# Score blocks of a head set further apart, priority for their maxima and exponentials, and one load for four output weight tiles

## The chip, the cores and the metric

The kernel runs on one core of a Trainium2 chip. The metric is device time in microseconds for one launch. The kernel before was timed three times: 1888.44, 1889.13 and 1891.86 us, median 1889.13. One further execution was profiled: 1886.52 us, of which the profile's span covers 1884.7 us.

## The reference, cut to what matters

A two-layer backbone processes 512 latent tokens and 128 context tokens with the same weights. Layer 0 is a state-space mixer and a gated convolutional feed-forward; layer 1 is differential attention and a second feed-forward. The change concerns the attention of layer 1 and its output projection:

```python
qp, kp, vp = diff_qkv(hp, att_qkv_w[slot])                 # 128 context tokens, 8 heads, 2 maps of 64
qs, ks_, vs = diff_qkv(hs, att_qkv_w[slot])                # 512 latent tokens
qs = rope_2d(qs, tabs); ks_ = rope_2d(ks_, tabs)
k_all = jnp.concatenate([cache_k[:, slot], ks_], axis=1)   # 640 keys
...
s = jnp.einsum('bqhcd,bkhcd->bhcqk', qi, k, preferred_element_type=F32) * DA_SCALE   # per block of 128 queries
p = jax.nn.softmax(s, axis=-1)
w = p[:, :, 0] - lam * p[:, :, 1]
return jnp.einsum('bhqk,bkhd->bqhd', w.astype(v.dtype), v)
...
o = (_rms(o) * subln_g.astype(F32) * (1.0 - lam_init)).astype(o.dtype)
return o.reshape(b, l, D_MODEL) @ out_w
```

Everything is float32 and has to keep nearly that precision: each large product is made of three matmuls, high part by high part, high by low, low by high.

## The kernel before, in words

**Tiles.** Activations lie with features on the 128 partitions and the 640 tokens (512 latent, then 128 context) along the row; 1024 features are 8 feature tiles. A dense output tile (`dense`, L153) takes 48 matmuls: for each of 8 feature tiles three products (`wh` by `h` high, `wh` by `h` low, `wl` by `h` high), each in two pieces of 256 and 384 columns. After each feature tile `hook` (L76) advances the clock of ticks by one and lets the pending side tasks (Python generators) emit their next piece. A generator says with `yield n` how many ticks it wants to wait. So the text of the program is: dense tiles of the weights in one fixed sequence, and between their feature tiles whatever side task is due. A scheduler then orders each engine's instructions from that text: it keeps dependencies and prefers what came earlier in the text, or what stands under a priority block, among what it takes to be ready. Each engine then runs its list strictly from front to back.

**Weights.** `prefetch` (L119) loads weight units of up to 1024 columns into four buffers; `cast` (L127) makes the high part `whi` on ACT and the low part `wlo` on DVE, one unit ahead of its use, in three rotating buffers. `whi` of a unit can only be written when the unit three earlier has been read for the last time.

**One head.** For head `hd` the dense sequence has the tiles q, k and v (`attention`, L1160). The three tiles of head 0 are computed together beforehand (`start_tiles`, tile name `st`). ACT copies each out of PSUM (`att_evac` L1025, `att_v` L993), DVE rotates q and k (`att_rope`). `att_head` (L1060) then computes the context scores (tile `sp`, 128x128 for two maps) and four score blocks of 128 queries by 640 keys for two maps (tile `sl`, 12 matmuls). For each map DVE takes the row maximum (`sm`, L1070), ACT the exponential (tile `e`), and `combine` joins both maps into weights `w`. `att_tail` (L1114) transposes the weights (`wpt`, `wt`), splits them into `wTh` on ACT and `wTl` on DVE, multiplies with the values (`ov`, `op`), squares the result (`osq`) and takes the sum of squares (`ms`).

**PSUM.** Six of eight banks form three slots of two banks (`psd`, L66). The dense tile in progress holds one. A score block takes the other two, one for each map, and gives each back when its exponential has read it. So a dense tile that begins while a block is held starts only when the first exponential is done, and a block starts only when both slots are free. `hold` (L1018) also makes the first matmuls of a block wait for the exponentials and copies noted in `self.held`.

**Spacing.** The ticks between blocks stand in `att_head`: after `combine` of the context scores 5 (L1092; 3 in the last head), then after each block 2, and between blocks 1, 3 and 1 (L1111), so that blocks start 3, 5 and 3 ticks apart. `attention` drains the task of the previous head after the k tile (L1170): what is left of it is emitted there without further dense tiles between.

**After the heads.** `project_out` makes the first 768 input features of the first five output tiles (weights of 768 columns), and `project_last` (L289) the rest of these five (256 columns each, one load and one cast for each tile) and the last three full tiles. `attention` passes `range(6, 8)` as `ks` there. The second feed-forward follows with `start_tiles`.

Of the kernel before, what the change touches and what calls it, by code (L numbers as in the profile page):

```python
# [18 lines left out]
P = 128  # L19
D = 1024  # L20
# [25 lines left out]
class Step:  # L46
# [72 lines left out]
    def prefetch(self, upto):  # L119
        while len(self.wraw) <= min(upto, len(self.units) - 1):  # L120
            u = len(self.wraw)
            ap, n = self.units[u]
            r = self.pw.tile([P, 1024], F32, tag="raw", name=f"raw{u}", bufs=RAW)
            self.nc.sync.dma_start(r[:, :n], ap)
            self.wraw[u] = r
# [163 lines left out]
    def project_last(self, h, ks, g, nextnorm, ks_last=None, parts="AB"):  # L289


        self.norm_begin()
        for i in range(KT - 3):
            ps = self.dense_ps("po")
            self.dense(ps, self.nextw(), ks, h)
            for hf in "AB":
                self.gate_add(i, ps, g, hf)
                self.norm_sq(i, hf)
        ks = ks_last or ks
        if self.modtask:  # L300
# [671 lines left out]
    def att_consts(self, pool):  # L972
# [4 lines left out]
        lv = t([P, 256], "lv")  # L977
        nc.sync.dma_start(lv, a["lam"])
        ls = t([P, 2], "ls")
        lj = t([P, 64], "lj")  # L980
# [6 lines left out]
        nc.vector.tensor_scalar(self.nlam, self.nlam, -LAM_INIT, None, ALU.add)  # L987
        self.sg = t([P, 2], "sg")
        nc.sync.dma_start(self.sg[:, 1:], a["subg"])
        nc.vector.tensor_scalar(self.sg[:, 1:], self.sg[:, 1:], 1.0 - LAM_INIT, None, ALU.mult)  # L990
        nc.vector.tensor_scalar(self.sg[:, :1], self.sg[:, 1:], 3.0 / 8, None, ALU.mult)

    def att_v(self, ps, hd, vs, pool):  # L993

        nc = self.nc
        x = self.slot("f", f"v{hd}", bufs=NF)
        self.held["evac"] = self.act(x, ps[:, PO:PO + T], AF.Copy)
        hi = pool.tile([P, NCH, P], F32R, tag="vh", name=f"vh{hd}", bufs=2)
# [26 lines left out]
    def att_evac(self, ps, hd, name, pool):  # L1025

        x = self.slot("f", f"{name}{hd}", bufs=NF)[:, :TS]
        p = pool.tile([P, TP], F32, tag=f"{name}p", name=f"{name}p{hd}", bufs=2)
        self.act(x, ps[:, PO:PO + TS], AF.Copy)
        self.held["evac"] = self.act(p, ps[:, PO + TS:PO + T], AF.Copy, scale=DA_SCALE if name == "q" else 1.0)  # L1030
        return x, p
# [28 lines left out]
    def att_head(self, hd, qp, kp, qs, k, vs, o, pool):  # L1060
# [7 lines left out]
        def softmax(s, n, m, st):  # L1068
            e = self.slot("f", f"e{m}", bufs=NF)
            nc.vector.tensor_reduce(st[:, m:m + 1], s, AX.X, ALU.max, negate=True)  # L1070
            self.held["exp"] = self.act(e[:, :n], s, AF.Exp, bias=st[:, m:m + 1], accum_out=st[:, 2 + m:3 + m])
            return e
# [18 lines left out]
        combine(w, TP, *em, st)  # L1091
        yield 3 if last else 5  # L1092
        ws = []
        for b in range(4):
# [15 lines left out]
            if b < 3:  # L1110
                yield ((1, 1, 1) if last else (1, 3, 1) if hd else (1, 3, 3))[b]  # L1111
        self.tails[hd] = self.add(self.att_tail(hd, w, ws, vs, o, pool), 1 if last else 2)

    def att_tail(self, hd, w, ws, vs, os_, pool):  # L1114
# [11 lines left out]

        def av(kc, hi, lo):
            self.mm(py, vh[:, kc, :], hi, kc == 0, False)
            self.mm(py, vh[:, kc, :], lo, False, False)
# [3 lines left out]
        for kc in range(NCH):  # L1133
# [5 lines left out]
            self.act(hi, pm, AF.Copy)  # L1139
            self.tt(lo, pm, hi.bitcast(F32), ALU.subtract)  # L1140
            if prev:
                av(kc - 1, *prev)
            prev = hi, lo
            yield 1 if hd == 7 else 2
# [57 lines left out]
    def weight_units(self):  # L1202
# [29 lines left out]
    def run(self):  # L1232
# [27 lines left out]
        with tc.tile_pool(name="att", bufs=1) as pool:  # L1260
            self.att_consts(pool)
            self.attention(hs[2], norm(1, 1, hs[3]), pool)
# [105 lines left out]
```

## Time and profile before

| what | us |
|---|---|
| median of three runs | 1889.13 |
| profiled execution | 1886.52 |
| span of its profile | 1884.7 |
| PE busy / PEld (weight loads) busy | 1839.6 / 1744.8 |
| DVE busy / ACT busy | 1369.5 / 955.1 |
| attention, from the first q tile of head 1 to the end of `po` | 1050.65 to 1399.02 |

PE is the TensorE's stream of matmuls, PEld its weight loads, DVE the VectorE, ACT the ScalarE, SPq the queue from which loads are issued. Times within the span are microseconds from its start. In a timeline row the columns are start, duration, engine, source line, operation, out and in by tile name, shape and count; the bracket at the end is idle time of that engine before the row and what ended it. In a list of waits a row gives the waiting group, the group waited for, total us, how often, and the longest. In a table by stretches of time the columns are: the stretch, its length, busy time and instruction count of PE, PEld, DVE, ACT and POOL, the granted TensorE clock (1.00 is full), the share of the DMA engines and GB/s. Matmul rows are pipelined and overlap, so the time of a group is read from its start to the next group's start.

### The profile page before, as it was taken

To read this page: it belongs to the slowest core of one execution; us is meant where nothing else is said; L and a number is where in the kernel's file an instruction comes from. 1 tells how busy PE (TensorE), PEld (TensorE's weight loads), DVE (VectorE), ACT (ScalarE), POOL (GpSimd) and SP (SyncE) were. 2 spreads that over 40 slices of the span, in tenths; PEclk is the share of its full clock that TensorE was granted. 3 is DMA by queue.
4 is the path that set the end of the run, shared out by engine and by line. 5 is a ranking of instruction groups with operands and counts; after the bars stand their busy time and mean duration, and the time that the engine had idled before them with its cause. 6 is when DMAs were issued, how large, how long until landed. Compare 5 with 4: busy or idle time off the path is not lost.

```text
span 1884.7 us, 32852 instructions
## 1 busy us (share of the span) xinstructions
PE 1839.6 (98%) x13322; PEld 1744.8 (93%) x13322; DVE 1369.5 (73%) x2640; ACT 955.1 (51%) x1748; POOL 0.2 (0%) x4
## 2 busy tenths in 40 slices
PE   7999999999999999999999899999999999999997
PEld 5889999999899999999999888888899999999996
DVE  6699999999669999973556877778686543553554
ACT  3489697877336431441443555566456432441441
POOL 0000000000000000000000000000000000000000
PEclk9999999999999999999999899999999999999998
DMA  9836253436524557532222211111132222222211
GB/s 347 271 104 166 80 150 101 147 120 211 187 70 156 181 188 226 176 92 83 71 72 82 64 46 58 58 57 32 33 124 79 79 78 70 73 72 80 73 40 56
DMA packets 79727, 209.74 MB, mean 111 GB/s; under 512 B 9324, under 2 KB 16088, under 8 KB 79448
## 3 DMA queue, kind: packets, MB, share of 16 engines
q1 hardware_dynamic: 79000, 207.13, 34.6%
q8 instruction: 104, 1.70, 0.4%
q10 hardware_dynamic: 576, 0.52, 0.1%
q14 instruction: 47, 0.39, 0.1%
HBM read 201.66 MB, written 5.96 MB: 110 GB/s over the span
## 4 chain that ended last, share of the span: by engine, by line
PE 90%; DVE 5%; ACT 3%; DMA 2%; issue 1%; SPq 0%; DVEq 0%; ACTq 0%
PE up L104 31%; PE po L104 25%; PE z L104 6%; PE x L104 5%; PE st L104 5%; PE yp L104 3%; PE v L104 3%; PE q L104 3%; PE bc L104 3%; PE ov L104 1%; ACT e L95 1%; PE modrow L104 1%; PE in L104 1%; PE sl L104 1%; DVE sm L1070 1%; PE wt L1136 1%
## 5 line engine op out<-in xcount | busy, mean ns | idle before, releaser
L95 ACT ACTIVATE whi<-raw 128x1024 fp32r<-128x1024 f32 (+4 forms) x230 | 234.8, 1022 | 382.6 <-PE po L104 240.4
L101 DVE TENSOR_TENSOR wlo<-raw,whi 128x1024 fp32r<-128x1024 f32 (+3 forms) x229 | 269.5, 1177 | 169.6 <-ACT whi L95 164.7
L98 DVE SCALAR_TENSOR_TENSOR xr<-po,mod,xr 128x256 f32<-128x256 f32 (+2 forms) x231 | 88.8, 433 | 158.6 <-PE po L104 158.5
L104 PE MATMUL po<-mh,whi 128*128 128x256 f32 (+1 forms) x704 | 167.7, 310 | 0.0
L104 PE MATMUL po<-ml,whi 128*128 128x256 f32 (+1 forms) x704 | 167.4, 310 | 0.0
L104 PE MATMUL po<-mh,wlo 128*128 128x256 f32 (+1 forms) x704 | 167.2, 309 | 0.0
L104 PE MATMUL up<-h01h,wlo 128*128 128x256 f32 (+1 forms) x656 | 149.4, 309 | 0.0
L104 PE MATMUL up<-h11h,wlo 128*128 128x256 f32 (+1 forms) x656 | 149.4, 309 | 0.0
L104 PE MATMUL up<-h11h,whi 128*128 128x256 f32 (+1 forms) x656 | 149.4, 308 | 0.0
L104 PE MATMUL up<-h11l,whi 128*128 128x256 f32 (+1 forms) x656 | 149.3, 308 | 0.0
L104 PE MATMUL up<-h01h,whi 128*128 128x256 f32 (+1 forms) x656 | 149.3, 308 | 0.0
L104 PE MATMUL up<-h01l,whi 128*128 128x256 f32 (+1 forms) x656 | 149.3, 308 | 0.0
L104 PEld LDWEIGHTS po<-mh,whi 128*128 128x128 f32 x704 | 128.5, 188 | 0.6 <-ACT mh L95 0.4
L104 PEld LDWEIGHTS po<-mh,wlo 128*128 128x128 f32 x704 | 128.7, 188 | 0.0
L104 PEld LDWEIGHTS po<-ml,whi 128*128 128x128 f32 x704 | 128.5, 188 | 0.0
L104 PEld LDWEIGHTS up<-h11h,whi 128*128 128x128 f32 x656 | 119.3, 188 | 0.0
L104 PEld LDWEIGHTS up<-h01h,whi 128*128 128x128 f32 x656 | 119.3, 188 | 0.0
L104 PEld LDWEIGHTS up<-h01h,wlo 128*128 128x128 f32 x656 | 119.3, 188 | 0.0
L104 PEld LDWEIGHTS up<-h11l,whi 128*128 128x128 f32 x656 | 119.3, 188 | 0.0
L104 PEld LDWEIGHTS up<-h11h,wlo 128*128 128x128 f32 x656 | 119.3, 188 | 0.0
L104 PEld LDWEIGHTS up<-h01l,whi 128*128 128x128 f32 x656 | 119.2, 188 | 0.0
L98 DVE SCALAR_TENSOR_TENSOR ca<-uraw,fcw,ca 128x511 f32<-128x511 f32 (+1 forms) x176 | 85.2, 545 | 11.7 <-ACT ca L95 11.7
(497 smaller groups left out, 4327.7 us busy)
## 6 DMA issues: line engine op xcount, KB each, us to landing
raw<-in_w_up SPq DMA_DIRECT2D x88, 512.0 KB, 3.5
mw<-in_modT SPq DMA_DIRECT2D x48, 512.0 KB, 3.5
raw<-in_w_in SPq DMA_DIRECT2D x40, 512.0 KB, 5.0
rb<-rowd SPq DMA_DIRECT2D x40, 512.0 KB, 5.3
raw<-in_w_dn SPq DMA_DIRECT2D x32, 448.0 KB, 3.4
raw<-in_w_qkv SPq DMA_DIRECT2D x24, 512.0 KB, 3.6
mr<-in_mod SPq DMA_DIRECT2D x44, 256.0 KB, 5.9
mp<-in_modp SPq DMA_DIRECT2D x32, 256.0 KB, 5.4
```

The source lines that it names most:

```text
L95: return self.nc.scalar.activation(out, in_, func, **k)
L98: return self.nc.vector.scalar_tensor_tensor(out, in0, s, in1, op0, op1)
L101: return self.nc.vector.tensor_tensor(out, a, b, op)
L104: return self.nc.tensor.matmul(out, lhsT, rhs, start=start, stop=stop)
L1070: nc.vector.tensor_reduce(st[:, m:m + 1], s, AX.X, ALU.max, negate=True)
L1136: nc.tensor.transpose(pm[:, b * P:(b + 1) * P], ws[b][:, kc * P:(kc + 1) * P], self.ident)
```

## The change

Nothing of the arithmetic changes; instructions are moved.

- The ticks between blocks become 4, 4, 4 with the 2 after each block (six feature tiles apart) for heads 1 to 5; 3, 2, 2 for head 0, 2, 2, 2 for head 6, 1, 1, 1 for head 7. Head 0 waits 3 ticks in place of 5 after its context scores. The tail of heads 0 to 6 starts 4 ticks after the last block in place of 2.
- The task of the previous head is drained after the v tile, no longer after the k tile.
- Maximum and exponential of a block, and the copies of q, k, v out of PSUM, stand under `tc.high_priority()`.
- In the tail the first matmul of each product with the values also waits for `wTl`.
- The second part of the output weights comes in units of four tiles by 256 columns: two units (1024 and 256 columns) in place of five. All later units get numbers smaller by three.
- The attention's small constants are loaded before `start_tiles`, and the arithmetic on them is emitted after it.

```diff
@@ prefetch
-            self.nc.sync.dma_start(r[:, :n], ap)
+            dst = r[:, :n]
+            self.nc.sync.dma_start(dst.rearrange("p (i c) -> p i c", i=ap.shape[1]) if len(ap.shape) == 3 else dst, ap)
@@ project_last
-            self.dense(ps, self.nextw(), ks, h)
+            n = len(ks) * P
+            j = i % (1024 // n) if ks_last else 0
+            if j == 0:
+                w = self.nextw()
+            self.dense(ps, [t[:, j * n:(j + 1) * n] for t in w], ks, h)
@@ att_v
-        self.held["evac"] = self.act(x, ps[:, PO:PO + T], AF.Copy)
+        with self.tc.high_priority():
+            self.held["evac"] = self.act(x, ps[:, PO:PO + T], AF.Copy)
...
@@ att_head, softmax
-            nc.vector.tensor_reduce(st[:, m:m + 1], s, AX.X, ALU.max, negate=True)
-            self.held["exp"] = self.act(e[:, :n], s, AF.Exp, bias=st[:, m:m + 1], accum_out=st[:, 2 + m:3 + m])
+            with self.tc.high_priority():
+                nc.vector.tensor_reduce(st[:, m:m + 1], s, AX.X, ALU.max, negate=True)
+                self.held["exp"] = self.act(e[:, :n], s, AF.Exp, bias=st[:, m:m + 1], accum_out=st[:, 2 + m:3 + m])
@@ att_head
-        yield 3 if last else 5
+        yield 3 if last else 5 if hd else 3
...
-                yield ((1, 1, 1) if last else (1, 3, 1) if hd else (1, 3, 3))[b]
-        self.tails[hd] = self.add(self.att_tail(hd, w, ws, vs, o, pool), 1 if last else 2)
+                yield {0: (3, 2, 2), 6: (2, 2, 2), 7: (1, 1, 1)}.get(hd, (4, 4, 4))[b]
+        self.tails[hd] = self.add(self.att_tail(hd, w, ws, vs, o, pool), 1 if last else 4)
@@ att_tail
-        def av(kc, hi, lo):
-            self.mm(py, vh[:, kc, :], hi, kc == 0, False)
+        def av(kc, hi, lo, gate):
+            self.hold(self.mm(py, vh[:, kc, :], hi, kc == 0, False), [gate])
...
@@ attention
+        consts = self.att_consts(pool)
+        next(consts)
         o, tk, self.tails, self.held = [], [], {}, {}
         self.start_tiles(h)
+        next(consts, None)
...
-            if hd:
-                self.drain(tk[hd - 1])
             q = self.att_q(q, hd, pool)
...
             self.add(self.att_v(self.next_tile(h, "v"), hd, vs, pool), 1)
+            if hd:
+                self.drain(tk[hd - 1])
@@ weight_units
-        u += [(a["w_ao"][i, :, c:], D - c) for i in range(KT - 3)]
+        per = 1024 // (D - c)
+        u += [(a["w_ao"][i:j, :, c:].rearrange("i p c -> p i c"), (j - i) * (D - c))
+              for i in range(0, KT - 3, per) for j in (min(i + per, KT - 3),)]
```

The first place where instructions move is the PE's list around the last blocks of head 0, in the k and v tiles of head 1. Before, three of the four blocks stand close together at the end of the k tile; the names are those of the text above (`w` are the weights of a block, `kh`, `kl`, `qh`, `ql` the split keys and queries):

```order
L1119 MATMUL wpt<-cst,wp 128x128
L1136 MATMUL wt<-cst,w_11827 128x128
L104 MATMUL sl<-kh_11673,qh_11662 128x320 x4
L104 MATMUL sl<-kl_11674,qh_11662 128x320 x4
L104 MATMUL sl<-kh_11673,ql_11663 128x320 x4
L1136 MATMUL wt<-cst,w_11871 128x128
L104 MATMUL sl<-kh_11673,qh_11662 128x320 x4
L104 MATMUL sl<-kl_11674,qh_11662 128x320 x4
L104 MATMUL sl<-kh_11673,ql_11663 128x320 x4
L104 MATMUL v<-h10h_11216,whi_11772 128x256
L104 MATMUL v<-h10h_11216,whi_11772 128x384
```

Now the fourth block of head 0 stands alone at the very end of the v tile, right ahead of the q tile of head 2:

```order
L104 MATMUL v<-h10h_11230,wlo_11773 128x256
L104 MATMUL v<-h10h_11230,wlo_11773 128x384
L104 MATMUL sl<-kh_11673,qh_11662 128x320 x4
L104 MATMUL sl<-kl_11674,qh_11662 128x320 x4
L104 MATMUL sl<-kh_11673,ql_11663 128x320 x4
L104 MATMUL q<-h10h_11216,whi_11905 128x256
L104 MATMUL q<-h10h_11216,whi_11905 128x384
```

The blocks of head 0 have moved apart: behind the first stand 25 matmuls of the k tile, behind the second 12 of k and 16 of v, behind the third 32 of v.

The second place is the PE's list where the k tile of a head in the middle ends and its v tile begins. Before, the block there is the fourth of the previous head:

```order
L104 MATMUL sl<-kh_12801,qh_12790 128x320 x4
L104 MATMUL sl<-kl_12802,qh_12790 128x320 x4
L104 MATMUL sl<-kh_12801,ql_12791 128x320 x4
L104 MATMUL k<-h10h_11230,wlo_12919 128x256
L104 MATMUL k<-h10h_11230,wlo_12919 128x384
L1119 MATMUL wpt<-cst,wp 128x128
L1136 MATMUL wt<-cst,w_13018 128x128
L1136 MATMUL wt<-cst,w_13089 128x128
L1136 MATMUL wt<-cst,w_13156 128x128
L104 MATMUL v<-h10h_11216,whi_13101 128x256
```

Now it is the third:

```order
L104 MATMUL sl<-kh_12749,qh_12738 128x320 x4
L104 MATMUL sl<-kl_12750,qh_12738 128x320 x4
L104 MATMUL sl<-kh_12749,ql_12739 128x320 x4
L104 MATMUL k<-h10h_11230,whi_12878 128x256
L104 MATMUL k<-h10h_11230,whi_12878 128x384
L104 MATMUL k<-h10l_11231,whi_12878 128x256
L104 MATMUL k<-h10l_11231,whi_12878 128x384
L104 MATMUL k<-h10h_11230,wlo_12879 128x256
L104 MATMUL k<-h10h_11230,wlo_12879 128x384
L104 MATMUL ms<-osq,cst 32x160 x4
L1128 MATMUL wpt<-cst,wp 128x128
L104 MATMUL v<-h10h_11216,whi_13021 128x256
```

Between the block and the v tile now stand six matmuls of the k tile and the sums of squares, where two and the transposes stood. The fourth block has gone to the v tile, with nine matmuls of v behind it ahead of the next q tile.

The third place is ACT's list at the same spot. Before:

```order
L95 ACTIVATE whi_13344<-raw_13099 128x1024
L95 ACTIVATE wpT<-wpt 128x128
L95 ACTIVATE e_13182,sm<-sl,sm 128x640
L95 ACTIVATE e_13185,sm<-sl,sm 128x640
L95 ACTIVATE k_13205<-k 128x512
L95 ACTIVATE kp_13206<-k 128x128
```

Now:

```order
L95 ACTIVATE osq<-o_12947 128x640
L95 ACTIVATE whi_13304<-raw_13019 128x1024
L95 ACTIVATE e_13139,sm<-sl,sm 128x640
L95 ACTIVATE e_13142,sm<-sl,sm 128x640
L95 ACTIVATE k_13153<-k 128x512
L95 ACTIVATE kp_13154<-k 128x128
L95 ACTIVATE wpT<-wpt 128x128
```

In both lists the two exponentials stand behind a cast of weights; only the copy `wpT` has moved behind them. In the v tile, where the fourth block now is, its first exponential stands ahead of the cast.

More of the change, by code (lines that the diff above doesn't have):

```diff
@@ L978, in att_consts @@
         nc.sync.dma_start(lv, a["lam"])
+        self.sg = t([P, 2], "sg")
+        nc.sync.dma_start(self.sg[:, 1:], a["subg"])
+        yield
         ls = t([P, 2], "ls")
@@ L987, in att_consts @@
         nc.vector.tensor_scalar(self.nlam, self.nlam, -LAM_INIT, None, ALU.add)
-        self.sg = t([P, 2], "sg")
-        nc.sync.dma_start(self.sg[:, 1:], a["subg"])
         nc.vector.tensor_scalar(self.sg[:, 1:], self.sg[:, 1:], 1.0 - LAM_INIT, None, ALU.mult)
@@ L1028, in att_evac @@
         p = pool.tile([P, TP], F32, tag=f"{name}p", name=f"{name}p{hd}", bufs=2)
-        self.act(x, ps[:, PO:PO + TS], AF.Copy)
-        self.held["evac"] = self.act(p, ps[:, PO + TS:PO + T], AF.Copy, scale=DA_SCALE if name == "q" else 1.0)
+        with self.tc.high_priority():
+            self.act(x, ps[:, PO:PO + TS], AF.Copy)
+            self.held["evac"] = self.act(p, ps[:, PO + TS:PO + T], AF.Copy, scale=DA_SCALE if name == "q" else 1.0)
         return x, p
@@ L1069, in softmax @@
             e = self.slot("f", f"e{m}", bufs=NF)
-            nc.vector.tensor_reduce(st[:, m:m + 1], s, AX.X, ALU.max, negate=True)
-            self.held["exp"] = self.act(e[:, :n], s, AF.Exp, bias=st[:, m:m + 1], accum_out=st[:, 2 + m:3 + m])
+            with self.tc.high_priority():
+                nc.vector.tensor_reduce(st[:, m:m + 1], s, AX.X, ALU.max, negate=True)
+                self.held["exp"] = self.act(e[:, :n], s, AF.Exp, bias=st[:, m:m + 1], accum_out=st[:, 2 + m:3 + m])
             return e
@@ L1139, in att_tail @@
             self.act(hi, pm, AF.Copy)
-            self.tt(lo, pm, hi.bitcast(F32), ALU.subtract)
+            gate = self.tt(lo, pm, hi.bitcast(F32), ALU.subtract)
             if prev:
                 av(kc - 1, *prev)
-            prev = hi, lo
+            prev = hi, lo, gate
             yield 1 if hd == 7 else 2
@@ L1260, in run @@
         with tc.tile_pool(name="att", bufs=1) as pool:
-            self.att_consts(pool)
             self.attention(hs[2], norm(1, 1, hs[3]), pool)
```

## Prediction

> **What bounds the kernel now.** The page comes first: who is busy, and on which engine the chain that ended last runs.
>
> ```profile
> span 1884.7 us, 32852 instructions
> PE 1839.6 (98%) x13322; PEld 1744.8 (93%) x13322; DVE 1369.5 (73%) x2640; ACT 955.1 (51%) x1748; POOL 0.2 (0%) x4
> PE 90%; DVE 5%; ACT 3%; DMA 2%; issue 1%; SPq 0%; DVEq 0%; ACTq 0%
> ```
>
> PE sets the time nearly everywhere. The change leaves its matmuls as they are, so it can only win time in which PE waits, or runs at a reduced clock. The second view is the table by stretches, cut at the starts of q tiles: first the stretch in which head 0's blocks run (q, k, v of head 1), then three of the five heads that follow, each from its q tile to the next, then windows of 4 us at the dips of the clock.
>
> ```profile
> 1050.65:1091.62 40.97, 34.27 (x226) 30.93 (x226) 30.46 (x59) 22.50 (x49) 0.00 (x0) 0.88 0.22 71
> 1128.36:1165.08 36.72, 34.94 (x248) 30.79 (x248) 28.36 (x58) 22.44 (x48) 0.00 (x0) 1.00 0.19 59
> 1165.08:1203.36 38.28, 36.51 (x249) 32.33 (x249) 28.46 (x58) 22.43 (x48) 0.00 (x0) 0.96 0.18 55
> 1240.08:1278.34 38.26, 36.48 (x249) 32.31 (x248) 28.44 (x58) 22.42 (x48) 0.00 (x0) 0.96 0.15 46
> 1072.00:1076.00 4.00, 2.37 (x13) 1.75 (x13) 4.00 (x6) 1.79 (x3) 0.00 (x0) 0.57 0.06 16
> 1076.00:1080.00 4.00, 1.79 (x12) 1.57 (x12) 3.30 (x7) 3.01 (x6) 0.00 (x0) 0.50 0.42 131
> 1080.00:1084.00 4.00, 4.00 (x20) 3.90 (x19) 2.22 (x5) 2.31 (x5) 0.00 (x0) 0.65 0.00 0
> 1188.00:1192.00 4.00, 2.40 (x20) 1.68 (x17) 3.88 (x5) 3.42 (x8) 0.00 (x0) 1.00 0.32 82
> 1192.00:1196.00 4.00, 4.00 (x19) 4.00 (x18) 3.84 (x9) 1.61 (x5) 0.00 (x0) 0.57 0.46 147
> 1332.00:1336.00 4.00, 4.00 (x27) 2.81 (x24) 2.44 (x3) 2.53 (x6) 0.00 (x0) 0.58 0.16 49
> ```
>
> Two equal heads differ by 38.28 - 36.72 = 1.56 us and by the clock alone (0.96 against 1.00). The third view is PE's list of waits for the same three parts: head 0's stretch (three rows), the five heads to 1278.34 (three rows), the rest up to 1400.
>
> ```profile
> PE sl L104 <- ACT e L95: 3.3, 2, 2.9
> PE sl L104 <- ACT kp L95: 1.9, 1, 1.9
> PE wt L1136 <- ACT wpT L95: 1.4, 1, 1.4
> ...
> PE v L104 <- ACT e L95: 4.6, 5, 0.9
> PE wt L1136 <- ACT wpT L95: 3.4, 5, 0.7
> PE sl L104 <- ACT e L95: 0.9, 5, 0.2
> ...
> PE po L104 <- ACT e L95: 1.2, 1, 1.2
> PE v L104 <- ACT e L95: 0.9, 1, 0.9
> PE op L104 <- DVE vl L101: 0.7, 1, 0.7
> PE po L104 <- ACT whi L95: 0.6, 1, 0.6
> PE po L104 <- DVE wlo L101: 0.6, 1, 0.6
> ```
>
> Nearly all of it is PE behind an exponential (`e`). The last view is the timeline of PE, ACT and DVE at one such place, the end of a k tile.
>
> ```profile
> 1148.09 0.46 PE L104 MATMUL k<-h10h,whi 128*128 128x256 f32 x2
> ...
> 1148.97 0.46 PE L104 MATMUL k<-h10h,whi 128*128 128x256 f32 x2
> ...
> 1150.79 0.57 PE L104 MATMUL sl<-kh,qh 64*128 64x320 f32 x4 [0.19 <-ACT e L95]
> ...
> 1151.87 0.56 PE L104 MATMUL k<-h10h,wlo 128*128 128x256 f32 x2
> 1152.27 0.27 PE L1119 MATMUL wpt<-cst,wp 128*128 128x128 f32 x1
> 1153.22 0.55 PE L1136 MATMUL wt<-cst,w 128*128 128x128 f32 x3 [0.68 <-ACT wpT L95]
> 1154.68 0.39 PE L104 MATMUL v<-h10h,whi 128*128 128x256 f32 x1 [0.91 <-ACT e L95]
> ...
> 1151.96 1.04 ACT L95 ACTIVATE whi<-raw 128x1024 fp32r<-128x1024 f32 x1
> 1152.90 0.26 ACT L95 ACTIVATE wpT<-wpt 128x128 f32<-128x128 f32 x1
> 1153.74 0.79 ACT L95 ACTIVATE e<-sl,sm 128x640 f32<-128x640 f32 x1 [0.57 <-DVE sm L1070]
> ...
> 1152.09 0.88 DVE L98 SCALAR_TENSOR_TENSOR w<-e,sm,e 128x640 f32<-128x640 f32 x1
> 1152.89 1.55 DVE L1070 TENSOR_REDUCE sm<-sl 128x1 f32<-128x640 f32 x2
> 1154.35 1.22 DVE L101 TENSOR_TENSOR wlo<-raw,whi 128x1024 fp32r<-128x1024 f32 x1
> ```
>
> Read from it: one feature tile (six matmuls) takes 1148.97 - 1148.09 = 0.88 us; a block holds PE 1151.87 - 1150.79 = 1.08. From the block's end to the v tile pass 2.81 us. Two k matmuls (0.40) and three transposes (about 0.3) fill 0.7, so 2.1 are lost, and 0.19 ahead of the block: 2.3 per head. The chain that ends the wait: DVE is busy with `w` until 1152.89, maximum, exponential 0.85 us later, its 0.79, and 0.15 to the matmul. If DVE and ACT are free at the block's end, the same chain takes about 0.1 + 0.85 + 0.79 + 0.15 = 1.9 us. That is the cover which any dense tile needs that starts behind a block.
>
> **The change, part by part.**
>
> *Head 0's blocks.* They now stand 25, 28 and 32 dense matmuls apart, 3.7 us or more at 0.88 per six; each needs 1.9 us and one more exponential before the next. The listed waits (3.3 + 1.9 + 1.4 = 6.6) go, and so does the reduced clock: 2.37 x 0.43 + 1.79 x 0.50 + 4.00 x 0.35 = 3.3 us. What is late next is the fourth block, at the very end of the v tile. It waits for the exponential of head 1's context scores; on ACT that one stands behind a cast whose buffer comes free two matmuls before the tile's end. The cast takes about 0.95 (next row on ACT), the short exponential about 0.4, the ways there and back 0.35, less the last 0.3 of the tile: 1.4. Then the q tile follows at once and lacks all of the 1.9. So 9.9 go and 3.3 come: **-6.6**. Ends: -9.9 if nothing new waits; -4.0 if the two new waits cost another 1 and a dip of 1.56.
>
> *The third block, at the end of the k tile, heads 2 to 6.* The cast still stands ahead of the exponential, and its buffer is free only when four of the six k matmuls behind the block are through: 0.2 to get going + 0.59, 0.19 to ACT (about 1.0 after the block), 0.95 for the cast, 0.79 and 0.15: the v tile starts 2.85 after the block. Six matmuls (1.1 with the 0.2), sums of squares and a transpose (about 0.45) fill 1.5. Left: 1.35, where 2.3 were. If the exponential came through first, it would be 1.9 - 1.5 = 0.4.
>
> *The fourth block, nine matmuls ahead of the q tile.* Its cover is 0.2 + 9 x 0.147 = 1.5 against 1.9, a new wait of 0.4. DVE may come late by a subtraction of 1.22 (the `wlo` row): up to 1.6.
>
> *The matmul held for `wTl`.* Behind it on PE stands the dense tile, so any wait there is PE's. The subtraction must now be done too, but 12 dense matmuls (1.76) have passed since its transposes. I take 0.25 per head, between 0 and 0.7.
>
> So a head in the middle loses 1.35 + 0.4 + 0.25 = 2.0, where it lost 2.3: -0.3 each, **-1.5** for five. Ends: 0.4 + 0.4 + 0.25, -1.25 each, -6.3; on the other side 1.35 + 1.6 + 0.7 = 3.65, +1.35 each, +6.8.
>
> *The dips.* Two of five heads ran at 0.96, 1.56 us each, right after a loss of 2.1 (busy 2.40 of 4.00, then clock 0.57). The largest single gap is now 1.35: **-3.1**; between -3.1 and 0.
> The Trainium skill, "TensorE: Matmul & The Clock Gate", Part 1 (the HAM clock gate), says that the clock halves after an idle window of about 3.4 us and asks for no PE gap over about 3 us. By it no dip would stem from these gaps, this term would be 0 and the sum 3.1 smaller; the rows at 1188 and 1192 show a dip after less idling than that, and the measurement decides.
>
> *The end of the attention.* The third block of head 7 was followed by `op` and a new `po` tile, waits 0.7 + 1.2, then a dip (0.58 in 4 us, 1.7). Now two `ov`, six dense matmuls and four transposes follow it, about 1.8 against 1.9. Up to 0.5 of wait stays; and one k tile end as above, -0.3. Together 3.6 - 0.5 + 0.3: **-3.4**, between -3.9 and 0.
>
> *The weights.* Five casts of 256 columns become one of 1024 and one of 256; that is work on ACT and DVE, off PE's path. The waits of `po` for `whi` and `wlo` (0.6 + 0.6) go, since the first full tile's cast now needs only the buffer of the last 768-column unit, free five output tiles earlier. But all later units move up by three: the second and third tile of the feed-forward fall into the buffers of the last two output tiles, which are free only at the end of the projection. Two subtractions of 1.22 then stand behind that end, where the first tile's 24 matmuls (2.9) cover: I take 1.0, between 0 and 2.5. Net **-0.2**, between -1.2 and +1.3.
>
> *Constants and queues.* The loads are issued in the same place, and no PE wait in the three lists is for a load; the tails' small transfers move with their tails, with a whole tile of slack: 0.
>
> Sum: 6.6 + 1.5 + 3.1 + 3.4 + 0.2 = 14.8. The profiled execution took 1886.52 (span 1884.7 and 1.8 around it), so 1871.7 for a run like it. It lay 2.6 under the median of the three runs, 1889.13; against that median the forecast is **1874.3**.
>
> **The rivals.** A change within 0.2%, 3.8 us, cannot be told from none by a measurement of this kernel.
>
> *A, slower.* ACT and DVE run their lists from front to back; priority changes places in the list, not what is ready. For it: in the row at 1152.90 `wpT` had waited behind the cast of 1.04, and PE for `wpT`. If the exponentials at all tile ends stand behind casts and the maxima behind subtractions of 1.22, a head loses 2.5 at the k end, 2.5 at the v end, 1.4 at the gate of the fourth block and 0.25: 6.65 instead of 2.3, +4.35 for five heads = +21.8, and the three heads without a dip get one (+4.7). With head 0's -6.6 that is +19.9: 1909. Against it: ACT's list has the fourth block's first exponential ahead of the cast. It decides from (6.6 + 3.4)/5 = 2.0 more per head than now, 4.3 in all.
> The Trainium skill says on the same page (Part 1, engine queue depths) that ACT and DVE are strict FIFO and only PE reorders, weight loads alone; the row at 1152.90 agrees.
>
> *B, only head 0 gains.* Priority is void at the k ends, the dips stay, the end of the attention trades its waits for others: -6.6, 1882.5. For it: the list on ACT still has the cast first. Against it: one long loss becomes three short ones.
>
> *C, no change.* The heads lose 1.3 more each (late DVE, as in the upper end), which eats head 0's gain: 1889. DVE is busy 28.4 of 36.7 us per head, so a shorter head leaves it less room.
>
> **How the numbers follow.** Forecast (1865 to 1880) 0.58, B 0.22, C 0.09, A 0.07, still better 0.04. Faster: 0.58 + 0.22 + 0.04 = 0.84; same 0.09; slower 0.07. The range holds the forecast, B and the edge of C: 1866 to 1886.
>
> **What would show it.** Right: the stretch from head 1's q tile to head 2's falls from 40.97 to about 32 (some tail work moves on); heads of 36 to 37 us with clock 1.00; PE waiting for `e` ahead of both v and q, about 1.4 and 0.4; the waits at `op` and `po` gone, a new one of about 1 at `st`. Wrong: heads over 38.5 us, waits of q or `sl` over 2 us in every head, or dips in more than two heads.

## The result and the profile after

| | before | after |
|---|---|---|
| median | 1888.95 (4 runs, 1888.44 to 1891.86) | 1879.82 (4 runs, 1879.43 to 1880.65) |
| profiled execution / its span | 1886.52 / 1884.7 | 1880.65 / 1878.9 |

The ratio is 0.9949, 95% interval 0.9932 to 0.9966: 9.1 us faster by the medians, where 14.8 were forecast. The page of the kernel after, the same three lines as before:

```profile
span 1878.9 us, 32832 instructions
PE 1838.2 (98%) x13322; PEld 1741.9 (93%) x13322; DVE 1369.5 (73%) x2637; ACT 952.9 (51%) x1745; POOL 0.2 (0%) x4
PE 91%; DVE 4%; ACT 3%; DMA 1%; issue 1%; SPq 0%; DVEq 0%; ACTq 0%
```

PE still sets the time. The table by stretches says where it changed: in three parts, from head 1's q tile to head 2's, the five heads to the last q tile, and from there to the end of the feed-forward's `st` tiles. Before, the second and third part (the first, 40.97, was shown):

```profile
1091.62:1278.34 186.72, 177.83 (x1237) 157.02 (x1237) 142.30 (x286) 112.16 (x236) 0.00 (x0) 0.98 0.18 55
1278.34:1422.56 144.22, 139.45 (x991) 126.77 (x990) 110.41 (x245) 78.85 (x153) 0.00 (x0) 0.99 0.21 62
```

After, all three parts, then two of the five heads alone:

```profile
1053.41:1085.78 32.37, 28.43 (x207) 25.66 (x206) 28.78 (x53) 19.77 (x43) 0.00 (x0) 1.00 0.30 100
1085.78:1270.29 184.51, 177.68 (x1236) 155.44 (x1237) 141.05 (x284) 111.31 (x236) 0.00 (x0) 0.99 0.16 52
1270.29:1416.00 145.71, 140.72 (x1007) 127.79 (x1008) 112.88 (x247) 79.16 (x154) 0.00 (x0) 1.00 0.19 63
...
1085.78:1122.71 36.93, 36.48 (x249) 32.36 (x249) 25.43 (x52) 21.25 (x47) 0.00 (x0) 0.96 0.12 40
...
1159.76:1196.57 36.81, 35.28 (x247) 30.78 (x247) 28.59 (x57) 22.43 (x48) 0.00 (x0) 1.00 0.18 58
```

Together 371.91 became 362.59, -9.3. The parts aren't work of the same size: the first has 226 - 207 = 19 fewer matmul records, the third 16 more. That is tail work that has moved on, three groups of transposes and two of products. A row of before gives their price:

```profile
1129.24 0.60 PE L1136 MATMUL wt<-cst,w 128*128 128x128 f32 x4
1129.59 0.48 PE L104 MATMUL ov<-wTh,vh 128*128 128x512 f32 x1
...
1130.37 0.45 PE L104 MATMUL q<-h10h,whi 128*128 128x256 f32 x2
```

3 x 0.35 + 2 x 0.78 = 2.6. So head 0's stretch won 8.6 - 2.6 = 6.0, the five heads 2.2, the last part lost 1.5 and, less what moved in, won 1.1. The waits of PE in the same three parts:

```profile
PE q L104 <- ACT e L95: 1.8, 1, 1.8
PE sl L104 <- ACT e L95: 1.2, 1, 1.2
PE v L104 <- ACT e L95: 0.8, 1, 0.8
...
PE q L104 <- ACT e L95: 3.1, 5, 1.8
PE wpt L1128 <- DVE rs_v L178: 1.8, 4, 0.4
PE v L104 <- ACT e L95: 1.8, 4, 0.4
PE ov L104 <- DVE wTl L101: 1.3, 4, 0.3
...
PE obc L104 <- DVE rs_y L98: 1.5, 1, 1.5
PE ms L104 <- ACT sq L95: 1.1, 1, 1.1
PE po L104 <- ACT e L95: 1.0, 2, 0.7
```

In head 0's stretch only the two forecast waits are left and one of 0.8. (The five of q in the second list include the 1.8 of the first: the wait ends where that window begins.) In the heads every wait is now below 0.5, but four of the five heads have four of them each; the first of the five (1085.78 to 1122.71) has none of these. The timeline at the end of a k tile, the place that the prediction worked out:

```profile
1183.87 0.46 PE L104 MATMUL sl<-kh,ql 64*128 64x320 f32 x4
1184.25 0.56 PE L104 MATMUL k<-h10h,whi 128*128 128x256 f32 x2
1185.14 1.06 ACT L95 ACTIVATE whi<-raw 128x1024 fp32r<-128x1024 f32 x1 [1.43 <-PE k L104]
1186.11 0.78 ACT L95 ACTIVATE e<-sl,sm 128x640 f32<-128x640 f32 x1
1186.26 0.33 PE L1128 MATMUL wpt<-cst,wp 128*128 128x128 f32 x1 [0.45 <-DVE rs_v L178]
1187.03 0.56 PE L104 MATMUL v<-h10h,whi 128*128 128x256 f32 x2 [0.44 <-ACT e L95]
```

The block ends at 1184.25, the cast stands ahead of the exponential on ACT, and the v tile starts 2.78 after the block (forecast 2.85). But of these 2.78 PE waits only 0.45 and 0.44, where the forecast had 1.35 for this place.

### The profile page after: what moved, and what is told of

Same layout as the page of the kernel before. It is cut to its first block, busy times and chain, and to the rows that moved or that the text cites. A ratio compares the mean times of both kernels' runs of the same rounds, so it can differ in the third digit from the quotient of the medians.

```text
span 1878.9 us, 32832 instructions
## 1 busy us (share of the span) xinstructions
PE 1838.2 (98%) x13322; PEld 1741.9 (93%) x13322; DVE 1369.5 (73%) x2637; ACT 952.9 (51%) x1745; POOL 0.2 (0%) x4
## 4 chain that ended last, share of the span: by engine, by line
PE 91%; DVE 4%; ACT 3%; DMA 1%; issue 1%; SPq 0%; DVEq 0%; ACTq 0%
PE up L104 31%; PE po L104 25%; PE z L104 6%; PE x L104 5%; PE st L104 5%; PE bc L104 3%; PE yp L104 3%; PE q L104 2%; PE v L104 2%; PE k L104 1%; PE modrow L104 1%; PE sl L104 1%; PE in L104 1%; ACT whi L95 1%; ACT e L95 1%; PE ov L104 1%
## 5 line engine op out<-in xcount | busy, mean ns | idle before, releaser
L95 ACT ACTIVATE whi<-raw 128x1024 fp32r<-128x1024 f32 (+3 forms) x227 | 234.2, 1033 | 387.2 <-PE po L104 239.6
L101 DVE TENSOR_TENSOR wlo<-raw,whi 128x1024 fp32r<-128x1024 f32 (+2 forms) x226 | 269.2, 1192 | 172.2 <-ACT whi L95 165.1
```

Source lines behind the costliest of these rows:

```text
L95: return self.nc.scalar.activation(out, in_, func, **k)
L101: return self.nc.vector.tensor_tensor(out, a, b, op)
```

## The experiments

Two theories were put to the test. The first is the prediction's account: every block needs about 1.9 us of other work on PE behind it, and the sum of uncovered waits and dips gives the time. The rivals give it all to one part: to priority, or to the spacing. The table has every kernel that ran: its median, its ratio to the kernel before in runs on the same chip, and the three parts in its profile. The kernel before took 1888.95, 1887.65, 1887.43 and 1886.30 in the four sets of runs, so medians of different rows can differ by 2 us for that reason alone; the ratios and the sums are the better comparison.

| kernel | median | ratio (95%) | head 0's blocks | five heads | last part | sum |
|---|---|---|---|---|---|---|
| before | 1888.95 | 1 | 40.97 | 186.72 | 144.22 | 371.9 |
| before once more | 1887.1 (1 run) | | 41.30 | 186.80 | 143.00 | 371.1 |
| after | 1879.82 | 0.9949 (0.9932 to 0.9966) | 32.37 | 184.51 | 145.71 | 362.6 |
| after once more | 1876.43 (1 run) | | 32.38 | 184.72 | 145.03 | 362.1 |
| head 0's spacing only | 1880.86 | 0.9964 (0.9950 to 0.9978) | 32.70 | 188.91 | 142.31 | 363.9 |
| priority only | 1878.37 | 0.9951 (0.9939 to 0.9964) | 40.23 | 180.13 | 142.30 | 362.7 |
| after without priority | 1896.87 | 1.0049 (1.0034 to 1.0064) | 32.74 | 199.63 | 148.87 | 381.2 |
| after, heads 1 to 6 narrow | 1875.20 | 0.9933 (0.9921 to 0.9946) | 32.40 | 185.29 | 141.55 | 359.2 |
| after, old weight units | 1879.24 | 0.9956 (0.9942 to 0.9970) | 32.39 | 184.71 | 145.48 | 362.6 |
| after, casts apart | 1879.82 | 0.9958 (0.9945 to 0.9972) | 32.38 | 184.80 | 144.97 | 362.2 |
| after, no hold on `wTl` | 1878.33 | 0.9959 (0.9946 to 0.9971) | 32.39 | 183.89 | 145.69 | 362.0 |
| after, head 0 early | 1875.28 | 0.9935 (0.9923 to 0.9948) | 29.99 | 185.20 | 144.44 | 359.6 |
| narrow and head 0 early | 1870.02 | 0.9917 (0.9903 to 0.9930) | 29.99 | 181.37 | 141.95 | 353.3 |
| the same with 1, 2, 1 ticks | 1871.88 | 0.9921 (0.9908 to 0.9935) | 29.97 | 181.61 | 144.29 | 355.9 |

**The two kernels once more.** No edit. Of the kernel before:

> The kernel before once more, unchanged, for a second profile. In the two profiles at hand the first st tile of the attention starts at 1026.50 (before) and 1029.33 us (after), though nothing ahead of it differs in the code. If that is the spread between executions, this profile has it anywhere from 1026 to 1030, and the stretches between q tiles repeat to 0.3 us: 41.0 for head 0's blocks, 36.7 for a head without a dip, 38.3 for one with. If the change lengthens what lies ahead, it is at 1026.5 again. If the dips hang on the phase of the execution and not on the place, they lie in other heads, and the number of them may differ.

Of the kernel after:

> The kernel after once more, unchanged, for a second profile. Expected: the stretches between q tiles repeat to 0.2 us (32.4 for head 0's blocks, 36.8 to 37.1 for the others), no dip in the middle heads, st to up at 25.5 as in the first profile. If st to up comes out at 24 or less, the wait there hangs on the execution and not on the numbers of the units.

Before once more, the five heads: two dips again, but in the second and the fourth of them, where the first profile had them in the third and the fifth.

```profile
1129.33:1167.57 38.24, 36.45 (x248) 32.29 (x248) 28.46 (x58) 22.45 (x48) 0.00 (x0) 0.96 0.19 56
1167.57:1204.30 36.73, 34.95 (x248) 30.80 (x248) 28.38 (x58) 22.44 (x48) 0.00 (x0) 1.00 0.18 58
1204.30:1242.60 38.30, 36.52 (x249) 32.34 (x248) 28.47 (x58) 22.45 (x48) 0.00 (x0) 0.96 0.18 56
1242.60:1279.34 36.74, 34.97 (x248) 30.80 (x248) 28.37 (x58) 22.44 (x48) 0.00 (x0) 1.00 0.15 48
```

So the place of these dips belongs to the execution. The number isn't fixed either: the dip near 1332 of the first profile isn't there in the second (1.00 in these 4 us, 0.58 in the first), and the last part is 1.2 shorter. The attention's first `st` tile starts at 1026.50 and 1027.03 in the two profiles of before, at 1029.33 and 1025.86 in those of after. The window from 20 to 30 us of after, first and second profile:

```profile
20.00:30.00 10.00, 8.28 (x109) 6.62 (x105) 7.66 (x13) 3.56 (x7) 0.00 (x0) 0.83 1.04 385
```

```profile
20.00:30.00 10.00, 8.45 (x118) 6.93 (x121) 7.74 (x16) 4.38 (x8) 0.00 (x0) 1.00 1.05 387
```

So a dip in the opening comes and goes in the same kernel. It explains a part of the difference of 3.5, about 8.28 x 0.17 = 1.4 by this window; the rest wasn't traced. With these shifts ahead of the attention the first pair of spans differs by 5.8 and the second by 1885.3 - 1874.6 = 10.7. The sums in the table leave it out; they repeat to 0.8. The second reading of `st` to `up` (24.84, the up tiles at 1412.29 less 1387.45) lies between both cases expected.

**Spacing without priority.** The three blocks `with self.tc.high_priority()` are taken out of the kernel after, what stands in them stays:

```diff
-            with self.tc.high_priority():
-                nc.vector.tensor_reduce(st[:, m:m + 1], s, AX.X, ALU.max, negate=True)
+            nc.vector.tensor_reduce(st[:, m:m + 1], s, AX.X, ALU.max, negate=True)
```

> The kernel after without its three priority blocks; the spacing of the blocks stays. In the instruction lists the fourth block of heads 1 to 5 then slips to the very end of the v tile. Account by terms (cover against a chain of 1.9 us): each q tile waits 1.9 instead of 0.34 in five heads, about +7.7, and where PE idles that long a dip can return: 1886 to 1889. Rival, the spacing alone brings the time and priority nothing: 1880. Rival, priority alone brings it: 1889 or more, and head 0's blocks alone (next run) bring nothing.

Slower than the kernel before by 0.49%, and slower than after by 17 us (by the ratios 19). First the wait of the q tiles of heads 2 to 6 (the first of the five ends where the window begins), then the timeline at one of them:

```profile
PE q L104 <- ACT e L95: 13.2, 5, 2.7
```

```profile
1165.00 0.46 PE L104 MATMUL sl<-kh,ql 64*128 64x320 f32 x4
...
1165.21 1.23 DVE L101 TENSOR_TENSOR wlo<-raw,whi 128x1024 fp32r<-128x1024 f32 x1 [0.82 <-ACT whi L95]
1166.35 1.55 DVE L1078 TENSOR_REDUCE sm<-sl 128x1 f32<-128x640 f32 x2
...
1167.20 0.79 ACT L95 ACTIVATE e<-sl,sm 128x640 f32<-128x640 f32 x1 [1.73 <-DVE sm L1078]
...
1168.14 0.57 PE L104 MATMUL q<-h10h,whi 128*128 128x256 f32 x2 [2.69 <-ACT e L95]
```

The fourth block has slipped to the end of the v tile, and there the subtraction of a cast (1.23) goes ahead of the maximum: the q tile waits 2.69, 0.8 more than the 1.9 expected, and four of the five heads have a dip. That is the prediction's rival A at one of its places (the maximum behind a subtraction), with -6 at head 0 and +13 in the five heads. The expected 1886 to 1889 was missed, because a bare chain was counted and no more than a dip or two.

**Each part alone.** The kernel before with head 0's spacing and drain, and nothing else:

```diff
-        yield 3 if last else 5
+        yield 3 if last else 5 if hd else 3
...
-                yield ((1, 1, 1) if last else (1, 3, 1) if hd else (1, 3, 3))[b]
+                yield ((1, 1, 1) if last else (1, 3, 1) if hd else (3, 2, 2))[b]
```

> The kernel before with only the spacing of head 0's blocks changed (3 ticks after its context scores, then 3, 2, 2, its task drained after the v tile); no priority, all other heads, the weights and the constants as before. Account by terms: head 0's stretch falls from 41.0 to about 34.5 (no tail work moved on, so less than 6.6 by how the lists fall without priority), the other heads and the end keep their waits and dips: 1882.5 to 1884. Rival, without priority head 0's blocks only trade their waits: 1886 to 1889.

The kernel before with the three priority blocks, and nothing else (the edit above, reversed):

> The kernel before with nothing but the three priority blocks added (maxima and exponentials, copies of q, k, v); all spacings, weights and constants as before. In ACT's list both exponentials at the end of a k tile now stand ahead of the cast of weights. Account by terms: the loss there falls from 2.3 to 1.3 to 1.5 per head in the five middle heads (chain of 1.9 less 0.7 of cover, 0.19 ahead), -0.8 to -1.0 each, and with it the two dips of 1.5 go: -7 to -8, head 0's stretch stays at 41: about 1881. Rival, priority is worth something only with the wide spacing: within 2 of the kernel before, 1887.6.

Head 0 alone brings 0.36%, priority alone 0.49%, as much as the whole change. Both came out faster than expected. Head 0's stretch fell to 32.70 where about 34.5 had been expected, because tail work did move on (211 matmul records in it, 226 before). With priority alone the five heads are 6.6 shorter, nearly as expected, and the other two parts are shorter too, by 0.7 to 1.1 and 0.7 to 1.9, which the account didn't have. Both rivals that give it all to one part fall, and the narrow spacing doesn't take priority's worth away. What priority does at the end of a k tile with the narrow spacing, by the timeline:

```profile
1187.07 0.56 PE L104 MATMUL k<-h10h,whi 128*128 128x256 f32 x2
...
1188.21 1.55 DVE L1073 TENSOR_REDUCE sm<-sl 128x1 f32<-128x640 f32 x2
...
1189.06 0.79 ACT L95 ACTIVATE e<-sl,sm 128x640 f32<-128x640 f32 x1 [0.77 <-DVE sm L1073]
...
1189.85 0.27 ACT L95 ACTIVATE wpT<-wpt 128x128 f32<-128x128 f32 x1
1190.00 0.56 PE L104 MATMUL v<-h10h,whi 128*128 128x256 f32 x2 [0.80 <-ACT e L95]
```

No cast stands ahead of the exponential any more, and the block itself has moved up: 1.86 of k matmuls follow it (1187.07 to 1188.93), where 0.40 did. The v tile waits 0.80. But from the block's end to the v tile pass 2.93 (1187.07 to 1190.00), no less than the 2.81 before: the maximum starts only 1.14 after the block. At this place priority gave the block more cover and didn't make its chain shorter. The rows of one head with priority alone (no dip in any of the five):

```profile
1164.34:1200.47 36.13, 35.12 (x249) 30.81 (x248) 28.13 (x57) 22.35 (x49) 0.00 (x0) 1.00 0.18 59
```

PE idles 36.13 - 35.12 = 1.01 in it, 1.78 before (36.72 - 34.94), 1.53 after (36.81 - 35.28).

**After with the narrow spacing in heads 1 to 6.**

```diff
-                yield {0: (3, 2, 2), 6: (2, 2, 2), 7: (1, 1, 1)}.get(hd, (4, 4, 4))[b]
-        self.tails[hd] = self.add(self.att_tail(hd, w, ws, vs, o, pool), 1 if last else 4)
+                yield {0: (3, 2, 2), 7: (1, 1, 1)}.get(hd, (1, 3, 1))[b]
+        self.tails[hd] = self.add(self.att_tail(hd, w, ws, vs, o, pool), 1 if last else 4 if hd == 0 else 2)
...
+            if hd > 1:
+                self.drain(tk[hd - 1])
```

(and the drain after the v tile for head 0 alone)

> The kernel after, but heads 1 to 6 with the narrow spacing again (1, 3, 1 ticks, tail after 2, the task of the previous head drained after k); head 0, priority, weights and constants stay as after. Account by terms: the wide spacing of the middle heads is worth only what it adds to priority: with priority alone a middle head loses about 1.4 in place of 2.3, with the wide spacing 2.1 in the listed waits and 0.3 in a more broken sequence on PE, so this kernel is 0 to 4 faster than the kernel after: 1876 to 1880. Rival, the wide spacing is what removes the dips: two or more dips of 1.5 come back and the heads lose 2.3 again: 1882 to 1885.

1875.2, a little under the expected 1876 to 1880. Against after it is 3.0 faster by the ratios (the two intervals overlap), and by the profiles' sums 359.2 against 362.1 to 362.6. So with priority the wide spacing of the middle heads, with the later tails and drains that belong to it, costs about 3 us. The two kernels with head 0 early, below, differ in the same edit: 353.3 against 359.6, by the ratios 3.4. Without priority, and with the small parts of the change, it cost some 17 (381.2 against 363.9, head 0's spacing alone).

**Head 0's blocks earlier.**

```diff
-                yield {0: (3, 2, 2), 6: (2, 2, 2), 7: (1, 1, 1)}.get(hd, (4, 4, 4))[b]
+                yield {0: (2, 2, 1), 6: (2, 2, 2), 7: (1, 1, 1)}.get(hd, (4, 4, 4))[b]
```

> The kernel after with head 0's blocks at 2, 2, 1 ticks in place of 3, 2, 2, so that the last one lies within the v tile and none right ahead of head 2's q tile. Account by terms: the waits of sl (1.2) and q (1.83) go, one of up to 1 comes at the earlier blocks: -2, about 1878. Rival, every block costs its chain somewhere in this stretch, and the waits only move: 1880.

1875.28, 4.5 less than after by the medians; the ratios give 2.6 (the intervals overlap) and the profiles' sums 2.5 to 3.0, where -2 was expected. The new wait of q had a price that the prediction didn't see. Three windows of the kernel after, at that wait and behind it:

```profile
1084.00:1086.00 2.00, 0.22 (x1) 0.22 (x2) 1.54 (x2) 1.56 (x4) 0.00 (x0) 0.89 0.66 205
1086.00:1088.00 2.00, 2.00 (x8) 2.00 (x9) 0.48 (x3) 1.81 (x4) 0.00 (x0) 0.50 0.18 66
1088.00:1090.00 2.00, 2.00 (x11) 1.86 (x10) 0.73 (x1) 0.00 (x0) 0.00 (x0) 0.75 0.00 0
```

A dip: 2.00 x 0.50 + 2.00 x 0.25 = 1.5 lost, and both profiles of the kernel after have it. So have the profiles of the two weight kernels and of the one without the hold, below (clock 0.95 to 0.96 in the head behind it). With the blocks earlier the same stretch runs at 1.00. But a wait has moved as well, as the rival said: the q tile of head 3 now waits 1.6, without a dip behind it. Head 0's stretch and the head behind it took 69.3 to 69.4 and now take 67.9; so the edit's own place gives 1.4 to 1.5. Most of the rest lies in the last part (144.44, after 145.71 and 145.03), where the wait of `ms` at the `st` tiles isn't listed this time; the edit gives no reason for that.

**The weights.** In one kernel the second part of the output weights comes in five units again (`j = 0` and the old list of units), in the other only the choice of the buffer is as if the numbers hadn't changed:

```diff
-            wp, t, b = (self.pw, "w", 3) if self.px is None or u % 5 < 3 else (self.px, "x", 2)
+            wp, t, b = (self.pw, "w", 3) if self.px is None or (u + 3 * (u > 140)) % 5 < 3 else (self.px, "x", 2)
```

> The kernel after, but with the second part of the output weights in five units of 256 columns again (so the units of the feed-forward have their old numbers). Account by terms: the stretch from the feed-forward's first st tile to its up tiles falls from 25.5 to about 23.5, the two waits of po for whi and wlo (0.6 each) come back, net -0.8: about 1879. Rival, the larger unit helps as the prediction had it (-0.2 net): 1880.

> The kernel after, but the casts of the feed-forward's second and third tile go to the same fresh buffers as before the units were renumbered (three is added to the unit's number in the choice of the buffer). Account by terms: the stretch from st to up falls from 25.5 to 23.5, and nothing comes back elsewhere: -1.5 to -2, about 1878. Rival, the stretch was longer for another reason (order of the squares on ACT): 1880.

In both the wait of `ms` at the `st` tiles (1.1, and 0.5 in the second profile of after) is gone, and `st` to `up` takes 23.53, as before. But the time doesn't fall: from the last q tile to the first `st` tile pass 121.95 and 121.44, where after has 120.22 and 120.19. With the casts apart the subtraction of the last output tile's weights is waited for instead, a row that isn't in after's list of waits:

```profile
PE po L104 <- DVE wlo L101: 0.6, 1, 0.6
```

Neither edit is worth anything that could be measured here. The first, 1879.24, fits both of its cases; the second is a miss: something did come back elsewhere.

**The hold on `wTl`.**

```diff
-            self.hold(self.mm(py, vh[:, kc, :], hi, kc == 0, False), [gate])
+            self.mm(py, vh[:, kc, :], hi, kc == 0, False)
```

> The kernel after without the extra hold of the first product with the values on wTl. In PE's list only the place of some ov matmuls changes. If the hold is the 0.33 per head that is listed at ov in the kernel after, the five middle heads gain 0.3 each: -1.6, about 1878. Rival: the next product needs wTl anyway and the pieces of PE's list stay as short, so the wait only moves: 1880.

The listed wait of `ov` is gone, and the five heads are 0.6 to 0.8 shorter, half of what was expected. The times don't tell it from nothing: the median is 1878.33 for 1879.82, but the ratio is 0.9959 for 0.9949.

**Both findings together.** The narrow spacing of heads 1 to 6 and 2, 2, 1 for head 0; then 1, 2, 1 in place of 1, 3, 1 as well.

> Both findings together: priority with the narrow spacing in heads 1 to 6 and head 0's blocks at 2, 2, 1 ticks (weights, constants and hold as after). Account by terms, from the kernel with the narrow spacing (1875.2): head 0's stretch and the next fall by 2, as they did between the kernel after and the one with head 0 early (1.6 to 2.4 in the stretches): about 1873. Rival: the late drain of head 0 makes the next head pay for it: 1875.

> As the last one, but 2 ticks in place of 3 between the second and third block of heads 1 to 6. In PE's list 18 matmuls of the k tile now stand behind the fourth block in place of 12, and the transpose of the context weights comes later. With the narrow spacing and priority the v tile starts 2.9 after that block's end, with 1.86 of cover, so it waits 0.8 to 1.0 per head; with 2.65 of cover 0.2 to 0.3 is left: -0.6 in each of six heads, about 1870. Rival: the blocks are then too close for ACT and DVE, and the wait goes to the third block: same as the last one.

1870.02 beats before by 0.83% and after by more than their intervals; it is the fastest kernel here, 3 us under the expected 1873. The account had left out a dip. In the kernel with the narrow spacing and head 0 as in after, the clock falls behind head 0's last block:

```profile
1083.00:1087.00 4.00, 2.17 (x10) 2.06 (x9) 1.98 (x5) 3.38 (x7) 0.00 (x0) 0.66 0.41 135
1087.00:1091.00 4.00, 4.00 (x18) 3.67 (x19) 0.89 (x1) 0.00 (x0) 0.00 (x0) 0.50 0.00 0
```

That is 2.17 x 0.34 + 4.00 x 0.50 = 2.7 lost. With head 0 early all three parts run at 1.00, and the sum falls by 5.9 (by the ratios 3.0).

The last kernel can't be told from it. In its profile the later heads are the shortest of all, 35.43 where 1, 3, 1 has 36.17, nearly the expected 0.6 less. But it pays elsewhere: the first two heads are 1.0 and 1.3 longer (with 8 matmul records more in the second), and there is a dip at the last head (first the later head, then the dip).

```profile
1157.27:1192.70 35.43, 35.00 (x249) 30.74 (x248) 28.17 (x57) 22.16 (x48) 0.00 (x0) 1.00 0.18 60
```

```profile
1314.00:1318.00 4.00, 2.60 (x10) 1.89 (x9) 3.17 (x7) 2.73 (x7) 0.00 (x0) 0.76 0.01 3
1318.00:1322.00 4.00, 4.00 (x24) 2.83 (x24) 2.44 (x7) 0.83 (x1) 0.00 (x0) 0.50 0.51 145
```

## Why the prediction was right in direction and too large

The direction, the chain behind a block and the two new waits at head 0 were right; the sum was -14.8 and the profiles show -9.0 to -9.3. The steps that failed are the end of the attention and the dips: of the 5.5 that are missing in the first profiles, the end with the weights was taken 2.5 too large, the dips 1.5, the middle heads 0.9 and head 0 0.6. Point by point:

- **Head 0's blocks, -6.6: -6.0 in its stretch.** The waits at the end, 1.2 and 1.83, were forecast as 1.4 and 1.9; the one of 0.8 at v wasn't foreseen. But the step "the q tile follows at once and lacks all of the 1.9" stopped there. By the prediction's own reading of the dips, a loss of that length can cost a dip of 1.5 behind it, and it did. That belongs to the term of the dips.
- **The dips, -3.1: -1.6.** The two in the middle heads went, as forecast; the new one came. The step that failed is "The largest single gap is now 1.35": it looked at the middle heads only, while the part on head 0's blocks had just made a gap of 1.9.
- **The middle heads, -0.3 each: +0.1 to +0.3 each in four of the five.** PE's idle time per head fell from 1.78 to 1.53, which is the forecast 0.3, but partly by luck. Both levels were about 0.5 too high. Before, a head lost 0.19 + 0.68 + 0.91 = 1.78 and not 2.3, because more than the reckoned 0.7 of work stood behind the block (2.81 - 0.68 - 0.91 = 1.22). After, it waits 0.44 at v (forecast 1.35), 0.3 at q (0.4), 0.33 at `ov` (0.25) and 0.45 at `wpt` for `rs_v`, a wait that the account didn't have: 1.5 and not 2.0. And its busy time rose from 34.94 to 35.28 for the same matmuls, and the account had no such term. In PE's list the dense runs have become shorter, with single transposes and products between them; that these switches cost the 0.34 is read from the traces and was not tested by itself. Without the hold on `wTl` the busy time stays up, so it isn't the hold. The first of the five heads, without its dip, is 1.3 shorter, and so the five together come to -3.1 + 1.5 + 0.7 - 1.3 = -2.2.
- **The end of the attention, -3.4, and the weights, -0.2: -1.1 together by the first profiles, -0.6 by the second.** The waits at `op` and for `whi` and `wlo` went, but an unforeseen one came, `obc` behind `rs_y` (1.5). There 14 dense matmuls stand between the sums of squares and `obc`, where before stood 21, and on DVE three updates of `xr` stand between the steps of the norm; neither was tested by itself. All listed waits of that part add up to 4.6 before and 5.1 after. The dip of 1.7 that this term also took as a gain wasn't in the second profile of before. The new wait at the `st` tiles came at 1.1 and 0.5 (forecast 1.0), though through the casts on ACT that stand ahead of the squares, not through the subtractions; the two weight kernels show the net of the whole edit to be about 0.
- **Rival A** was a real one: at the ends of the v tiles it is what the kernel does without priority, and the time of that kernel, 1896.87, is nearer to 1909 than to the forecast. What held it off is that the fourth block's maximum and exponential came ahead of the cast, as the order showed. Without priority that block also stands at the very end of the tile, so the run doesn't separate its place from the order on DVE and ACT.
- **Rival B, only head 0 gains, 1882.5:** its time was close, its mechanism not. Against the mean of the two profiles of before, head 0 alone gives -7.6 in the sums, priority alone -8.8, both with the narrow heads -12.3; the wide spacing then gives about 3 back. The forecast took the wide spacing for a gain of 0.3 per head, because it compared it with the heads before and not with priority at the narrow spacing.

The Trainium skill, "TensorE: Matmul & The Clock Gate", Part 1 (the HAM clock gate), calls the activity window free-running and its effect at warm-up variable from run to run. The dips here, though they aren't at warm-up, vary likewise: they changed heads between two profiles of one kernel. The same part of the Trainium skill has the clock halve after an idle window of about 3.4 us. That differs from these traces: dips followed single waits of 0.9 to 2.7 us, and not every time.

## What to carry to other kernels

Price a moved wait with what follows it: a gap that can drop the clock costs its length and the dip behind it, and the account of dips has to go through every gap that the change makes, not only those it mends. When a change has several parts, ask what each is worth beside the others: here priority removed what the wide spacing was also meant to remove, and the spacing's own small waits (and perhaps its shorter runs, not tested) were left as a cost. And take two profiles before a term of 1 to 3 us is built on one place: some dips wander between executions.

## What was not expected of the hardware

The length of a wait alone doesn't decide whether the clock drops. In the kernel without priority the q tile at 1168.14 waits 2.69 and the one at 1127.79 only 2.37, and it is the shorter wait that a reduced clock follows, 0.60 (each time the window that ends with the wait, then the next):

```profile
1166.00:1170.00 4.00, 1.86 (x12) 1.86 (x13) 3.22 (x7) 2.79 (x6) 0.00 (x0) 1.00 0.66 209
1170.00:1174.00 4.00, 4.00 (x33) 3.62 (x33) 2.72 (x4) 1.42 (x4) 0.00 (x0) 1.00 0.01 4
1125.00:1129.00 4.00, 1.63 (x14) 1.37 (x13) 3.13 (x11) 2.55 (x7) 0.00 (x0) 0.97 0.43 136
1129.00:1133.00 4.00, 4.00 (x24) 3.67 (x23) 1.77 (x2) 0.82 (x2) 0.00 (x0) 0.60 0.30 82
```

The second of these has another wait close by: PE had waited 1.09 just ahead of the block that precedes it, so that 3.5 us of idling lie within 4.6. The plainer case is four equal waits in the same profile. The q tiles at 1168.14, 1207.01, 1247.37 and 1287.77 all waited 2.69, and in the 4 us from each of them the clock was 1.00, 0.57, 0.61 and 0.68. The dip behind head 0 in the kernel after, which all six profiles with these waits have, also follows two waits, 1.20 and 1.83 with one block between them; whether the sum of the waits or their place in time decides, no run here separates.

And one kernel, twice run, can differ by 3.5 us (1029.33 and 1025.86) before the code that is under study begins.
